# Local attention's probabilities scaled by ScalarE instead of VectorE, with a new table for the order of the work, in a two-layer fp32 trunk

## The chip, the cores and the metric

The kernel runs on one core of a Trainium2 chip. Its engines are TensorE (PE in the profile, with its weight loads as PEld), VectorE (DVE), ScalarE (ACT), GpSimd (POOL) and SyncE (SP), which issues the transfers. The metric is device time in microseconds for one execution, as the median of several runs.

## The reference

Two decoder layers over a sequence of 1024 positions and a width of 1024, all in float32. Each layer normalises, projects once, gives the parts of the projection to four token mixers of 256 channels, normalises their outputs, projects out, adds, and then runs a gated feed-forward part:

```python
h = rmsnorm(x, attn_norm[l])
proj = h @ w_in[l]          # split into the inputs of four mixers
y_a = mla_attention(...)    # causal latent attention, 4 heads, rotary part
y_b = short_gated_conv(...)
y_c = multiscale_pool(...)
y_d = swa_sink_attention(q_sw, k_sw, v_sw, swa_sinks[l], slopes)
...                         # per-group rmsnorm, mixed
x = x + mixed @ w_o[l]
h2 = rmsnorm(x, ffn_norm[l])
gate, up = jnp.split(h2 @ w_gate_up[l], 2, axis=-1)
x = x + (jax.nn.silu(gate) * up) @ w_down[l]
```

The scaling that the change touches is the division in the softmax of `swa_sink_attention`: four heads with two key and value heads, a window of 128 positions in blocks of 128, a bias that falls with distance, and one sink logit per head that takes part in the sum and is then dropped:

```python
p = softmax(concatenate([sc, sink], axis=-1), axis=-1)[..., :-1]
out = einsum('bnkgqs,bnskd->bnqkgd', p, vv)
```

## The kernel before

Everything is kept transposed, channels on partitions, and the 1024 positions are two halves of 512. A float32 product is three products of rounded halves: each operand is split into a high half, a cast by ScalarE (L305, L237 for weights), and a low half, a subtract by VectorE (L306, L238); the helper that issues the three products is at L294, so most matmuls carry that line whatever they belong to. Tiles called `u` live in numbered SBUF buffers (in `u40_2007` the buffer is 40, the tile 2007); `tp`, `tn`, `te`, `sm` are small pools of temporaries; `ps_mm`, `ps_s`, `ps_t`, `ps_pv` are PSUM tiles, where `ps_mm` has two buffers. A matmul that is first to read a buffer's new tile waits for the cast or subtract that wrote it, and that one waits for the last matmul that read the old tile.

The program runs layer by layer: input projection and the mixers (0 to about 430 us in layer 0, 1090 to 1500 in layer 1), the feed-forward's gate and up products (430 to about 815, 1500 to 1805), its down projection (815 to 1090, 1805 to 2022), and a short tail. Gate and up, down and input projections use seven products in place of eight on 2x2 blocks, so their operands are also summed by VectorE and GpSimd, and stored to and loaded from memory by SP.

Places that the prediction speaks of:
- `swa_unit` (L742): one unit is one of two key heads and one block of 128 queries, 32 units in all. TensorE makes the scores of two query heads (L753), VectorE adds the bias and takes the row maxima, ScalarE takes the exponentials and row sums, VectorE adds the sink's share and takes reciprocals, and then the rows `p3` are multiplied by their reciprocals `rs` (L791, two instructions a unit). TensorE transposes the result (L802), it is split by L305 and L306, and multiplied with the values (L814).
- `values()` of the latent attention (L1109 to 1156): four value tiles, each one `ps_mm` tile of 2 x 256 columns, filled by six products and then emptied in two halves by ScalarE (L1155) and VectorE (L1156).
- Key products into `ps_s`, score products (L1223 to 1225), their masking with row maxima on VectorE (L1231), normalisation by sums of squares (L355, L362 to L368, with a load of ScalarE's tables ahead of L362 and L363), accumulation in SBUF (L372), and copies out of PSUM by ScalarE (L458).

What sets the order: the whole program is first recorded, each instruction with its rank. `places` (L2346) groups instructions by engine and written tile, and adds to the rank of a group the number that the table `MOVES` (L2279) holds for it. `arrange` (L2138) then runs through the recorded steps as a list scheduler: an engine takes, of the instructions that it holds to be ready, the one with the lowest place. `order_engines` (L2359) fixes the resulting order on each engine. Each engine works strictly in that order, so an instruction that waits holds up those behind it.

Of the kernel before, what the change touches and what calls it, by code (L numbers as in the profile page):

```python
# [14 lines left out]
AF = mybir.ActivationFunctionType  # L15
ALU = mybir.AluOpType
# [106 lines left out]
def trunk_kernel(ctx: ExitStack, tc: tile.TileContext, ins, out):  # L123
    nc = tc.nc
    act, dve, pe, pool, sp = nc.scalar, nc.vector, nc.tensor, nc.gpsimd, nc.sync
# [450 lines left out]
    for l in range(L):  # L576
# [94 lines left out]
        if l == 0:  # L671
# [15 lines left out]
            if l == 0:  # L687
                enter_norm(1)
                dve.tensor_copy(e_r, cst[:, CC_E : CC_E + P])
                for i in range(L):  # L690
                    for o, c, n in ((nsink, PC_SINK, 4), (nffn, PC_FFN, NK)):
                        dve.tensor_scalar(
                            out=o[:, i * n : i * n + n],
# [48 lines left out]
        def swa_unit(g, i):  # L742
# [47 lines left out]
            for h in range(2):  # L790
                dve.tensor_scalar(  # L791
                    out=p3[:, h, c0:],
                    in0=p3[:, h, c0:],
                    scalar1=rs[:, h : h + 1],
                    scalar2=None,
                    op0=ALU.mult,
                )
# [1340 lines left out]
def arrange(steps, rank=lambda v: v.rank):  # L2138
# [368 lines left out]
```

## Time and profile before

| | |
|---|---|
| median of 3 runs | 2034.13 us (2032.77 to 2035.87) |
| the profiled execution | span 2031.1 us; no other time is given for it |
| mean granted TensorE clock | 0.998 |
| PE busy | 2014.0 us (99%) |
| DVE busy | 1644.2 us (81%) |
| ACT busy | 1030.7 us (51%) |
| POOL busy | 210.7 us (10%) |
| transfers | 320.21 MB |

The span runs from the first to the last instruction of one execution. Busy time is the sum of an engine's instructions; matmul ends are modelled, so that back-to-back matmuls overlap on the page, and a late start shows best as the distance between two starts. In rows of a timeline a bracket such as `[1.79 <-DVE u L1156]` is idle time of the engine ahead of the row and what ended it.

### The profile page before, as it was taken

What the parts mean: (1) busy time and instruction counts of PE and PEld (TensorE: products, weight loads), DVE (VectorE), ACT (ScalarE), POOL (GpSimd) and SP (SyncE); (2) the same over time, 40 slices, a digit from 0 to 9 for tenths busy, and PEclk for the clock granted to TensorE, in tenths of its full rate; (3) what the DMA queues carried; (4) which work ended last, traced back from release to release, by engine and by line L of the source; (5) the groups of instructions that cost most, each with busy time, mean ns of one, the idle gap of its engine ahead of it and who ended that gap; (6) DMA issues with size and microseconds to landing.
All of it is one profiled execution on the core that took longest, in us unless ns stands there. A gap on an engine that the chain in (4) does not pass through costs nothing.

```text
span 2031.1 us, 26457 instructions
## 1 busy us (share of the span) xinstructions
PE 2014.0 (99%) x9378; PEld 1669.4 (82%) x9378; DVE 1644.2 (81%) x2793; ACT 1030.7 (51%) x1803; POOL 210.7 (10%) x212
## 2 busy tenths in 40 slices
PE   9999999999999999999999999999999999999998
PEld 7887888878888888888888878888888888888887
DVE  7889989998888888655778999899977777886555
ACT  7447656763333335443545676667333233355342
POOL 0000000013212213000000000000322222220000
PEclk9999999999999999999999999999999999999999
DMA  5100223346666667875455112231644454497652
GB/s 185 55 27 34 75 87 111 126 141 228 211 217 228 217 232 256 304 241 174 148 176 167 39 41 99 89 127 58 218 161 145 159 182 147 157 325 261 198 175 88
DMA packets 163781, 320.21 MB, mean 158 GB/s; under 512 B 13248, under 2 KB 85056, under 8 KB 163648
## 3 DMA queue, kind: packets, MB, share of 16 engines
q1 hardware_dynamic: 163648, 318.51, 45.6%
q8 instruction: 74, 1.21, 0.2%
q14 instruction: 59, 0.48, 0.1%
HBM read 220.41 MB, written 98.04 MB: 157 GB/s over the span
## 4 chain that ended last, share of the span: by engine, by line
PE 93%; DVE 3%; ACT 2%; DMA 1%; issue 1%; SPq 0%; DVEq 0%; ACTq 0%
PE ps_mm L294 37%; PE ps_s L294 28%; PE ps_t L294 11%; PE ps_pv L294 8%; PE ps_pv L1289 2%; PE ps_t L1277 2%; PE ps_s L1223 1%; PE ps_s L1224 1%; PE ps_s L1225 1%; PE ps_pv L814 1%; PE ps_s L753 1%; PE ps_mm L1109 1%; PE ps_t L802 1%; DVE u L346 1%; DVE u L306 1%
## 5 line engine op out<-in xcount | busy, mean ns | idle before, releaser
L294 PE MATMUL ps_mm<-u,u 128*128 128x512 f32 (+1 forms) x3402 | 856.6, 388 | 2.3 <-ACT u L237 1.3
L294 PEld LDWEIGHTS ps_mm<-u,u 128*128 128x128 f32 x3402 | 621.7, 188 | 126.8 <-issue 3.1
L294 PE MATMUL ps_s<-u,u 128*128 128x512 f32 x2628 | 651.2, 389 | 0.0
L294 PEld LDWEIGHTS ps_s<-u,u 128*128 128x128 f32 x2628 | 492.6, 188 | 104.2 <-DVE te L1796 0.8
L305 ACT CAST u<-u 128x1024 fp32r<-128x1024 f32 (+2 forms) x400 | 344.3, 883 | 412.1 <-PE ps_s L294 82.1
L306 DVE TENSOR_TENSOR u<-u,u 128x1024 fp32r<-128x1024 f32 (+2 forms) x400 | 412.7, 1049 | 165.2 <-ACT u L305 127.3
L172 POOL TENSOR_TENSOR u<-u 128x256 f32<-128x256 f32 x176 | 204.3, 1162 | 743.0 <-DMA u<-in_w_dn 239.2
L294 PE MATMUL ps_t<-u,u 128*128 128x512 f32 (+1 forms) x1142 | 275.1, 378 | 1.2 <-ACT u L305 0.8
L294 PEld LDWEIGHTS ps_t<-u,u 128*128 128x128 f32 x1142 | 205.5, 188 | 42.1 <-DVE u L306 1.3
L294 PE MATMUL ps_pv<-u,u 128*128 128x512 f32 x696 | 172.9, 389 | 0.0
L294 PEld LDWEIGHTS ps_pv<-u,u 128*128 128x128 f32 x696 | 130.5, 188 | 27.5 <-ACT tn L458 0.3
L1604 ACT ACTIVATE tp<-tp 128x512 f32<-128x512 f32 x84 | 53.3, 634 | 117.1 <-DVE tp L372 116.8
L1286 POOL MEMSET u<- 128x128 f32 x32 | 6.2, 220 | 858.8 <-DVE te L372 623.7
L305 ACT CAST u<-ps_t 128x512 fp32r<-128x512 f32 (+4 forms) x136 | 64.9, 507 | 58.7 <-PE ps_t L1277 34.1
L306 DVE TENSOR_TENSOR u<-ps_t,u 128x512 fp32r<-128x512 f32 (+4 forms) x136 | 77.0, 584 | 13.6 <-ACT u L305 12.7
L308 ACT ACTIVATE u<-u,par 128x512 fp32r<-128x512 f32 x100 | 70.0, 719 | 34.0 <-DVE u L372 10.9
L309 DVE SCALAR_TENSOR_TENSOR u<-u,par,u 128x512 fp32r<-128x512 f32 x100 | 73.1, 752 | 4.5 <-ACT u L308 4.4
L1605 DVE TENSOR_TENSOR tp<-tp,u 128x512 f32<-128x512 f32 x84 | 62.6, 745 | 13.2 <-ACT tp L1604 12.7
L340 ACT ACTIVATE tn<-u 128x512 f32<-128x512 f32 (+1 forms) x92 | 53.3, 594 | 39.0 <-DVE u L1882 30.2
L458 ACT COPY tn<-ps_s 128x512 f32<-128x512 f32 x66 | 38.4, 582 | 62.8 <-PE ps_s L294 62.5
L372 DVE TENSOR_TENSOR tp<-tp,u 128x512 f32<-128x512 f32 x80 | 60.9, 761 | 1.1
L1289 PE MATMUL ps_pv<-u,u 128*128 128x512 f32 (+2 forms) x184 | 54.4, 358 | 0.0
(220 smaller groups left out, 2171.9 us busy)
## 6 DMA issues: line engine op xcount, KB each, us to landing
u<-in_w_gu SPq DMA_DIRECT2D x88, 512.0 KB, 3.6
ad<-u SPq DMA_DIRECT2D x154, 256.0 KB, 2.8
u<-ad SPq DMA_DIRECT2D x70, 512.0 KB, 4.9
u<-in_w_dn SPq DMA_DIRECT2D x68, 512.0 KB, 4.9
qd<-u SPq DMA_DIRECT2D x44, 512.0 KB, 3.0
u<-qd SPq DMA_DIRECT2D x32, 512.0 KB, 4.9
u<-in_w_in SPq DMA_DIRECT2D x29, 512.0 KB, 3.5
u<-ws SPq DMA_DIRECT2D x28, 512.0 KB, 3.5
```

Source lines behind the costliest of these rows:

```text
L172: pool.tensor_tensor(out=o, in0=o, in1=u, op=ALU.add)
L294: pe.matmul(o, w, r, start=start and k == 0 and i == 0, stop=stop and k == n - 1 and i == 2, skip_group_check=again,)
L305: act.copy(hi, f)
L306: dve.tensor_tensor(out=lo, in0=f, in1=rd(hi), op=ALU.subtract)
L308: act.activation(hi, f, AF.Copy, scale=gain)
L309: dve.scalar_tensor_tensor(out=lo, in0=f, scalar=gain, in1=rd(hi), op0=ALU.mult, op1=ALU.subtract)
L340: act.activation(q, f, AF.Square)
L372: dve.tensor_tensor(out=o, in0=a, in1=b, op=ALU.mult)
L1277: pe.transpose(p[:, b * P : (b + 1) * P], pr[b][j // 4][:, (j % 4) * P : (j % 4 + 1) * P], ident,)
L1289: pe.matmul(py[:, c0:], v_of(j, h), R.ap(s)[:, c0:], start=j == 0 and n == 0, stop=j == nj - 1 and n == 1,)
L1604: last_silu = act.activation(g, g, AF.Silu)
L1605: dve.tensor_tensor(out=g, in0=g, in1=r, op=ALU.mult)
```

## The change

Two things are changed. In `swa_unit` the rows are multiplied by their reciprocals by a ScalarE activation with the function Copy and a scale per row, in place of VectorE's `tensor_scalar`, 64 instructions in all. And the table `MOVES`, 543 entries before, is replaced by one of 3856 entries that reach over the whole program. The number of matmuls (9352), transfers (830), table loads (11) and all other instructions is unchanged. Lines below the edit are four lower in the changed kernel: L1156 is L1152 there.

```diff
             for h in range(2):
-                dve.tensor_scalar(
-                    out=p3[:, h, c0:],
-                    in0=p3[:, h, c0:],
-                    scalar1=rs[:, h : h + 1],
-                    scalar2=None,
-                    op0=ALU.mult,
+                act.activation(
+                    p3[:, h, c0:], p3[:, h, c0:], AF.Copy, scale=rs[:, h : h + 1]
                 )
...
 MOVES = {
-    3: -1110, 4: -1104, 5: -984, 7: -776, 8: -1105, 14: -914, 15: -964, 16: -307, 18: -279, 20:
...
+    4736: 90, 4737: 227, 4738: -330, 4739: 202, 4740: 163, 4741: 10,
 }
```

What the table does is seen in the engines' orders. First VectorE at the value tiles of layer 0, around 218 to 224 us of the profile before (`ps_mm_2204` and `ps_mm_2216` are the first and second value tile). Before:

```order
L372 TENSOR_TENSOR te_2176<-ps_mm_2148,u30_302 128x512
L342 SCALAR_TENSOR_TENSOR u33_2070<-tn_2252,u33_2070 128x512
L238 TENSOR_TENSOR u21_2120<-u32_2117,u45_2119 128x768
L306 TENSOR_TENSOR u20_2256<-u33_2070,u20_2256 128x512
L372 TENSOR_TENSOR u27_2066<-u27_2066,te_2176 128x512
L1156 TENSOR_TENSOR u32_2203<-ps_mm_2204,u32_2203 128x4x64
L1156 TENSOR_TENSOR u7_2215<-ps_mm_2216,u7_2215 128x4x64
L372 TENSOR_TENSOR te_2192<-ps_s_2185,u39_1403 128x512
L1156 TENSOR_TENSOR u32_2203<-ps_mm_2204,u32_2203 128x4x64
```

Of the change:

```order
L372 TENSOR_TENSOR te_2176<-ps_mm_2148,u30_302 128x512
L342 SCALAR_TENSOR_TENSOR u33_2070<-tn_2252,u33_2070 128x512
L372 TENSOR_TENSOR u27_2066<-u27_2066,te_2176 128x512
L238 TENSOR_TENSOR u21_2120<-u32_2117,u45_2119 128x768
L306 TENSOR_TENSOR u20_2256<-u33_2070,u20_2256 128x512
L1152 TENSOR_TENSOR u7_2215<-ps_mm_2216,u7_2215 128x4x64
L372 TENSOR_TENSOR te_2192<-ps_s_2185,u39_1403 128x512
L1152 TENSOR_TENSOR u7_2215<-ps_mm_2216,u7_2215 128x4x64
L238 TENSOR_TENSOR vlo_2306<-vraw_2303,vhi_2305 128x256
L1152 TENSOR_TENSOR u32_2203<-ps_mm_2204,u32_2203 128x4x64
```

The two tiles were emptied in turn, the first one first; now the second is emptied, both halves, and then the first, whose other half follows three rows further on. In the changed program the third tile has the buffer of the second, and the fourth that of the first.

Second, ScalarE ahead of the feed-forward part of layer 0, around 410 to 418 us. `u24_4292` is the cast of a 128x1024 tile that products of the feed-forward read; the `L362` to `L364` rows normalise. Before:

```order
L362 ACTIVATE tn_4204<-ps_pv_4198 128x512
L305 CAST u22_4281<-tp_4273 128x512
L363 ACT_TABLE_LOAD
L363 ACTIVATE tn_4204<-tn_4204 128x512
L364 ACTIVATE tn_4205<-tn_4204 128x512
L305 CAST u32_2203<-tp_4274 128x512
L305 CAST u28_4285<-tp_4275 128x512
L466 ACTIVATE te_4325<-u29_3436,par_75 128x512
L305 CAST u24_4292<-u42_3928 128x1024
```

Of the change:

```order
L305 CAST u22_4281<-tp_4273 128x512
L362 ACT_TABLE_LOAD
L362 ACTIVATE tn_4204<-ps_pv_4198 128x512
L305 CAST u24_4292<-u42_3928 128x1024
L363 ACT_TABLE_LOAD
L363 ACTIVATE tn_4204<-tn_4204 128x512
L305 CAST u32_2203<-tp_4274 128x512
L364 ACTIVATE tn_4205<-tn_4204 128x512
```

The cast of `u24_4292` moves ahead of the table load of L363; `u32_2203` stands ahead of L364, but behind that cast.

Third, TensorE in the products with the weight halves `u36_2006` (high) and `u40_2007` (low), around 203 to 208 us. `u40_1944`, read by L355, is the tile that buffer 40 held before `u40_2007`. The change has:

```order
L355 MATMUL ps_t_1943<-u40_1944,ones_r_79 128x512
L294 MATMUL ps_mm_2035<-u29_248,u21_1862 128x512 x2
L294 MATMUL ps_mm_2035<-u29_248,u2_1863 128x512
L294 MATMUL ps_mm_2123<-u7_131,u36_2006 128x512 x2
L294 MATMUL ps_mm_2123<-u7_131,u40_2007 128x512
```

and before, the end of that stretch read:

```order
L294 MATMUL ps_mm_2035<-u28_244,u21_1862 128x512
L294 MATMUL ps_mm_2123<-u7_131,u36_2006 128x512 x2
L294 MATMUL ps_mm_2035<-u28_244,u21_1862 128x512
L294 MATMUL ps_mm_2035<-u28_244,u2_1863 128x512
L294 MATMUL ps_mm_2035<-u29_248,u21_1862 128x512 x2
L294 MATMUL ps_mm_2035<-u29_248,u2_1863 128x512
L294 MATMUL ps_mm_2123<-u7_131,u40_2007 128x512
```

The last L355 on `u40_1944` has moved back behind the products that stood after it: it is now six matmuls ahead of the first reader of `u40_2007`, where it had been 22.

507 rows, old and new, of the table MOVES are left out of this document.

## The prediction

> **What bounds the kernel now.** I read the page, then its chain of waits, then the busy times by stage, then the rows around every place where TensorE starts late.
>
> ```profile
> span 2031.1 us, 26457 instructions
> PE 2014.0 (99%) x9378; PEld 1669.4 (82%) x9378; DVE 1644.2 (81%) x2793; ACT 1030.7 (51%) x1803; POOL 210.7 (10%) x212
> ...
> PE 93%; DVE 3%; ACT 2%; DMA 1%; issue 1%; SPq 0%; DVEq 0%; ACTq 0%
> ```
>
> TensorE sets the end: busy for 99% of the span and 93% of the chain. A change that leaves the matmuls as they are, as this one does, can only move the late starts between them. They are counted against the step of an undisturbed run, here from the chain:
>
> ```profile
> 884.36 14.96 PE ps_mm L294 x66
> ```
>
> 14.96 / 66 = 0.2267 us from the start of one 128x512 matmul to the next. The windows by stage (after the length: busy time of PE, PEld, DVE, ACT, POOL; then the granted clock, which is full) show where idle time stands:
>
> ```profile
> 0.00:220.00 220.00, 217.68 (x1043) 180.35 (x1044) 189.27 (x415) 136.03 (x285) 0.55 (x6) 1.00 0.21 74
> 220.00:430.00 210.00, 207.28 (x1027) 171.76 (x1026) 194.48 (x409) 146.38 (x302) 2.69 (x14) 1.00 0.27 97
> 430.00:800.00 370.00, 369.70 (x1628) 304.79 (x1627) 317.54 (x430) 146.26 (x199) 92.49 (x80) 1.00 0.65 223
> 800.00:1100.00 300.00, 300.00 (x1363) 249.06 (x1362) 202.11 (x311) 144.41 (x233) 9.96 (x8) 1.00 0.63 209
> ```
>
> The feed-forward and down-projection of layer 0 (430 to 1100) have 0.30 us of PE idleness: nothing can be won there, only lost. Idle time, 2.3 and 2.7 us, stands in the entry and mixer stages ahead of them.
>
> **The change part by part: the scaling.** It removes 64 VectorE instructions and adds 64 on ScalarE.
>
> ```profile
> L791 DVE TENSOR_SCALAR tp<-tp,sm x64: 273/349/357, 60.8 to 1155.6; 128x256 f32<-128x256 f32 x56, 128x128 f32<-128x128 f32 x8
> ...
> who waited for it (us, times):
> ...
> L410 ACT ACTIVATE u<-u,par x8: 507/513/514, 1937.9 to 2021.3; 128x256 f32<-128x256 f32 x8
> ...
> 50.00:210.00 160.00, 160.00 (x787) 132.19 (x786) 140.06 (x331) 92.72 (x213) 0.00 (x0) 1.00 0.11 37
> 1090.00:1200.00 110.00, 109.97 (x536) 89.44 (x535) 106.94 (x249) 79.46 (x171) 0.00 (x0) 1.00 0.22 71
> ...
> 50.00:210.00 160.00, 9.48 (x32) 1.00 0.11 37
> 1090.00:1200.00 110.00, 6.63 (x22) 1.00 0.22 71
> ```
>
> VectorE sheds 64 x 0.349 = 22 us. The nearest ScalarE row, L410, an activation with a parameter on the same 128x256 shape, takes 0.51 us, so ScalarE takes on at most 64 x 0.51 = 33 us. The last two rows are L791's own share of the two stretches above them. In 1090 to 1200 VectorE falls from 106.94 to 100.3 of 110 us (97% to 91%) and ScalarE rises by 22 x 0.51 to 90.7 (82%); in 50 to 210 they go to 82% and 68%. Neither gets full. PE idles 0.03 us in these 270 us and nobody waited for L791, so alone this is worth little. A modelled matmul end (0.39 us long at a step of 0.2267) hides late starts under about 0.16 us, and those the relief of a 97% engine can shorten: I take 1.0 us won, between 2 us won and the loss of the third rival.
>
> **The order.** The table goes from 543 to 3856 entries; rows move on every engine. These are the late starts that it touches.
>
> ```profile
> 221.15 0.75 PE L355 MATMUL ps_t<-u,ones_r 128*128 128x512 f32 x2
> 223.69 0.36 PE L294 MATMUL ps_mm<-vhi,u 128*128 128x256 f32 x1 [1.79 <-DVE u L1156]
> ...
> 412.76 3.56 PE L294 MATMUL ps_s<-u,u 128*128 128x512 f32 x15
> 417.11 0.73 PE L294 MATMUL ps_t<-u,u 128*128 128x512 f32 x2 [0.79 <-ACT u L305]
> 417.68 0.86 PE L294 MATMUL ps_s<-u,u 128*128 128x512 f32 x3
> 418.68 1.19 PE L294 MATMUL ps_t<-u,u 128*128 128x512 f32 x4
> ...
> 445.12 1.52 PE L294 MATMUL ps_s<-u,u 128*128 128x512 f32 x6
> 446.48 0.61 PE L294 MATMUL ps_t<-u,u 128*128 128x512 f32 x2
> 447.37 0.97 PE L294 MATMUL ps_t<-u,u 128*128 128x512 f32 x3 [0.28 <-DVE u L306]
> ...
> 1416.74 2.20 PE L294 MATMUL ps_s<-u,u 128*128 128x512 f32 x9
> 1419.97 0.73 PE L294 MATMUL ps_mm<-u,u 128*128 128x512 f32 x2 [1.03 <-ACT u L305]
> 1420.54 0.62 PE L294 MATMUL ps_s<-u,u 128*128 128x512 f32 x2
> ```
>
> Start to start, less the steps between: at 221, 2.54 - 2 x 0.2267 = 2.09 us; at 412 to 418, 5.92 - 20 x 0.2267 = 1.39; at 445, 2.25 - 8 x 0.2267 = 0.44; at 1416, 3.23 - 9 x 0.2267 = 1.19. After such a stop the next start is late too (1419.97 to 1420.54 is 0.57 for two steps, 0.11 over); for the two not inside the sums I add 0.2.
>
> *What goes.* At 412 and 1416 the cast of a raw 128x1024 tile stood too far back in ScalarE's queue:
>
> ```profile
> 411.87 1.28 ACT L363 ACT_TABLE_LOAD   x1
> ...
> 414.37 1.13 ACT L305 CAST u<-tp 128x512 fp32r<-128x512 f32 x2
> ...
> 416.03 1.03 ACT L305 CAST u<-u 128x1024 fp32r<-128x1024 f32 x1
> ```
>
> The last row is the cast PE waited for. In the new order it stands ahead of the table load, so it passes 411.87 to 416.03, 4.16 us of work, three times the 1.39 lost: gone. At 1416 the PE rows that read the cast's result stand 60 and more matmuls further behind their neighbours, 13 us: 1.19 gone. At 445 nine ps_mm matmuls, 2.0 us, are put ahead of the one that waited 0.44: gone.
>
> *What stays.* At 221 the two orders look different, but the third value tile is held by the same kind of chain. VectorE began it when the last matmul of the product before had ended, and reached the emptying that PE waited for at the end of the second row:
>
> ```profile
> 218.53 0.69 DVE L372 TENSOR_TENSOR te<-ps_mm,u 128x512 f32<-128x512 f32 x1
> ...
> 223.13 0.42 DVE L1156 TENSOR_TENSOR u<-ps_mm,u 128x256 fp32r<-128x256 f32 x1
> ```
>
> That is 5.02 us. The new order empties the second tile first and gives its buffer to the third: the same queue less one L1156, about 4.7, against the same PE work between (6 key products, two value tiles, two L355). So the third tile gains 0.3, and the fourth now waits for L238, L1156, L306, L1257 and L1156, about 2.1 us, behind 2.0 us of PE work: 0.1 lost. I take 0.2 won of the 2.09.
>
> *What comes new.*
>
> ```profile
> 203.14 0.69 DVE L372 TENSOR_TENSOR u<-u,te 128x512 f32<-128x512 f32 x1
> 203.74 0.30 DVE L1231 CUSTOM_DVE_ANT_0 ps_s<-ps_s,cst 128x128 f32<-128x128 f32 x1
> ...
> 204.84 0.75 DVE L309 SCALAR_TENSOR_TENSOR u<-u,par,u 128x512 fp32r<-128x512 f32 x1
> 205.51 1.22 DVE L238 TENSOR_TENSOR u<-u,u 128x1024 fp32r<-128x1024 f32 x1
> ...
> 1412.63 0.61 ACT L305 CAST u<-tp 128x512 fp32r<-128x512 f32 x1
> ...
> 1089.25 0.59 ACT L458 COPY tn<-ps_mm 128x512 f32<-128x512 f32 x1 [1.29 <-PE ps_mm L294]
> ...
> 1090.36 0.94 PE L294 MATMUL ps_mm<-u,u 128*128 128x512 f32 x3
> ```
>
> - 203: u40_2007, the low half of a weight, is written over u40_1944. From the last reader of the one to the first of the other there were 22 matmuls; there are 6, 1.36 us. In VectorE's queue L372 (0.60 to the next start), the three L1231 (203.74 to 204.84, 1.10) and L238 (1.22) stand between: 2.9 us. Late by up to 1.6, or by 0 if VectorE's first rows run before; I take 1.2.
> - 412 again: the first of the two casts in the 414.37 row, which the product at 417.68 reads, stands behind the moved cast now. It ended at about 415.0; 1.03 more for the moved cast, 0.6 less for L364, which it passes, is 415.4. Its reader comes 6 matmuls (1.36) earlier, and 1.39 of stop ahead of it are gone: 414.9. Late by 0.5, and up to 0.9; I take 0.6.
> - 1090: L458's result was ready at 1089.84 for a product at 1090.36, 0.52 spare. The product comes 4 matmuls earlier (0.5 to 0.9 us) and L458 nine instructions later in its queue. Bounds 0 and 1.0; I take 0.5.
> - 1416 again: the cast at 1412.63, ready at 1413.24, is read by the seventh of the nine ps_s from 1416.74, at 1418.10. The reader moves 26 matmuls (5.9 us) earlier, to 1412.2, the cast two instructions back. Late by 1.0, bounds 0 and 2.2.
> - Tight buffers elsewhere. For each SBUF buffer I counted the matmuls from the last reader of its old tile to the first of its next. Below 12 there were 7 tiles and there are 40; 30 of them lie in the stages without idleness, where there was 1. An old site at distance 8 is inside this row:
>
> ```profile
> 1204.90 6.26 PE L294 MATMUL ps_mm<-u,u 128*128 128x512 f32 x26
> ```
>
> Undisturbed, 26 are 0.39 + 25 x 0.2267 = 6.06: it cost 0.20. The other six old sites show 0.07 together by the same count, so one costs 0.27 / 7 = 0.04, and 33 more 1.3 us; bounds 0 and 33 x 0.44 (the wait at 445) = 14.5.
>
> **Sum.** Gone: 1.39 + 0.44 + 1.19 + 0.2 + 0.2 + 1.0 = 4.4. New: 1.2 + 0.6 + 0.5 + 1.0 + 1.3 = 4.6. The span becomes 2031.1 + 0.2 = 2031.3. The median of the runs shown is 2034.1, 3.0 over the profiled span; with the same 3.0 the forecast is **2034.3 us**, no change.
>
> **Rivals.**
> 1. The new waits hardly come: every release behind them is at its early bound, since VectorE has 22 us less to do and ScalarE half its time free. Then the 4.4 stay won and of the 4.6 no more than 0.4 comes: 2034.1 - 4.0 = 2030.1, and with the 2 us bound of the relief 2029.1. For it: each of the four new waits is a small difference of two sums, while 445 and 1416 have four and ten times the cover they need. Against it: three of the four new places are late by the rows even if nothing else slips.
> 2. Tight buffers decide: slower. Place: 430 to 1100 and 1500 to 1990. At 8 matmuls, 1.81 us, a cast of 1.03 leaves 0.78; one other 128x1024 cast ahead of it in ScalarE's queue uses that up and 0.25 more, and VectorE's subtract, 1.22, waits behind. At 0.25 us for each of 33 sites 8.3 us are lost instead of 1.3: 2034.3 + 7.0 = 2041.3. It passes the margin from about 0.16 us a site. Against it: ScalarE is busy 146.26 of 370 us there.
> 3. ScalarE's longer scaling is late: slower. Each of 32 units takes 2 x (0.51 - 0.35) = 0.32 us more before its transposes; if PE waits in 20 of them, 6.4: 2034.3 + 6.4 = 2040.7. It passes the margin from 12 units. Against it: nobody waited for L791, beside a VectorE that was 97% busy. The Trainium skill (ScalarE: Activation LUTs, Rules for kernel authors) says that a multiply belongs on VectorE rather than ScalarE; the trace agrees on the price of one (0.51 against 0.349 us), and by that rule this rival's time would be the result.
>
> **How the numbers follow.** A difference under 0.2%, 4.07 us, cannot be told from no change: faster is below 2030.06, slower above 2038.2. The forecast has 0.50, its own range 2030.5 to 2038 (new waits at their bounds): 0.02 faster, 0.43 the same, 0.05 slower. Rival 1 has 0.29: 0.24 faster, 0.05 the same. Rival 2 has 0.12: 0.10 slower, 0.02 the same. Rival 3 has 0.05, slower, and 0.04 is left for a late load in the moved DMA queue, slower. Faster 0.26, same 0.50, slower 0.24. The range runs from 2028.5, just past rival 1, to 2039.5, which cuts off the upper half of rivals 2 and 3.
>
> **What the profile after will show.** Right: a wait of about 1.7 us for L1152 (once L1156) near 220 and new PE waits near 203, 412, 1087 and 1412 of 0.5 to 1.5 each, none of the old ones at 416, 446 and 1419; the scaling at about 0.51 us with nobody waiting. Rival 1: PE idleness of 0 to 430 under 3 us, where it was 5.0. Rival 2: over 3 us of PE idleness in 430 to 1100. Rival 3: PE waiting for the scaling or its transposes in 50 to 210. The forecast is wrong if the span leaves 2027 to 2035.

## The result, and the profile after

The changed kernel takes **2066.75 us** (2065.67 to 2070.15, four runs), beside 2033.50 us of the kernel before on the same chip: a ratio of 1.0163, 95% interval 1.0149 to 1.0177. It is slower by 33 us. The forecast was 2034.3 us, no change, in a range that ended at 2039.5: the result lies outside it.

The page of the changed kernel begins:

```profile
span 2068.4 us, 26441 instructions
PE 2029.0 (98%) x9378; PEld 1662.6 (80%) x9378; DVE 1627.1 (79%) x2729; ACT 1051.5 (51%) x1867; POOL 197.2 (10%) x212
```

The shares hardly move, and they are not where to look. VectorE's busy time falls by 17 us and ScalarE's rises by 21, the way that the scaling's move asks; the span grows by 37.3 us (the profiled execution of the change, 2070.15 us, is the longest of its four). TensorE's work is the same, so these are late starts. The busy times of the kernel before from 1500 on, which the prediction did not show (length: busy time of PE, PEld, DVE, ACT, POOL; granted clock; DMA share; GB/s):

```profile
1500.00:1800.00 300.00, 300.00 (x1324) 248.13 (x1323) 231.47 (x304) 107.32 (x148) 70.30 (x61) 1.00 0.48 167
1800.00:2031.00 231.00, 221.53 (x1100) 188.01 (x1098) 137.02 (x184) 95.14 (x135) 9.56 (x8) 0.99 0.59 205
```

and of the changed kernel:

```profile
220.00:430.00 210.00, 206.92 (x1020) 169.30 (x1019) 191.95 (x409) 144.20 (x298) 2.84 (x16) 1.00 0.29 97
430.00:800.00 370.00, 362.58 (x1578) 293.83 (x1577) 305.58 (x414) 139.20 (x191) 89.91 (x80) 1.00 0.63 210
800.00:1100.00 300.00, 295.73 (x1315) 241.93 (x1313) 196.79 (x282) 145.64 (x224) 9.41 (x8) 1.00 0.64 214
1500.00:1800.00 300.00, 299.56 (x1317) 246.36 (x1316) 224.61 (x295) 102.91 (x143) 62.77 (x59) 1.00 0.44 150
1800.00:2068.00 268.00, 252.77 (x1221) 209.73 (x1219) 162.81 (x218) 109.33 (x154) 12.55 (x14) 0.99 0.62 209
```

From 430 to 1100, where TensorE had 0.30 us of idleness, it now has 7.42 + 4.27 = 11.7. The modelled matmul ends hide part of each stop; from start to start, less the undisturbed step, the loss against the kernel before is 3.3 us in 0 to 430, **20.0 in 430 to 1100**, 3.0 in 1100 to 1500 and **11.6 from 1500 on**, 37.9 together. Where a stage is held to end moves the first three by a us or two. About four fifths lie in the feed-forward and down-projection stages.

What ends the idleness there is seen best in one piece of the chain of waits of the changed kernel (start, length, what):

```profile
984.87 2.06 PE ps_s L294 x9
986.93 0.02 issue
986.95 5.44 DMA u<-ad
992.38 0.02 issue
992.41 1.05 ACT u L305
993.46 0.04 issue
993.50 0.50 PE ps_s L294
```

A buffer came free with a product at 986.9; a load into it was issued at once, took 5.44 us, its cast followed within 0.03 us, and the product that reads the cast within 0.04. Nothing in this chain has any cover. In the kernel before the same load (`u24_8596`) landed at 947.72, its cast ended at 948.80 and its first reader started at 964.44, 15.6 us later.

Another piece shows a store in the load's place. Two rows of the changed kernel's timeline:

```profile
451.72 1.04 ACT L305 CAST u<-u 128x1024 fp32r<-128x1024 f32 x1 [6.99 <-DMA ad<-u]
452.81 0.73 PE L294 MATMUL ps_t<-u,u 128*128 128x512 f32 x2 [1.51 <-ACT u L305]
```

and of the kernel before, the same cast:

```profile
444.95 1.05 ACT L305 CAST u<-u 128x1024 fp32r<-128x1024 f32 x1 [2.03 <-DMA ad<-u]
```

The cast writes into a buffer from which a store into `ad` was still reading. In the changed kernel ScalarE is idle for 6.99 us ahead of it: it isn't busy, it waits for a transfer.

For each late start over 0.15 us I followed the waits, and the queue of the waiting engine, back to where the chain began. In the changed kernel 25 begin with a load (18.1 us), 13 with a store (9.5), 14 stand behind a long queue of VectorE or ScalarE work, fourteen steps and more (8.4); before it was 1 load (1.4), 2 stores (0.6), 9 queues (4.3). Where a chain is held to begin is in part a choice; followed in another way, single sums come out up to 4 us different, and the classes keep their order. So of the 38 us lost, 25.6 begin with a transfer and some 4 with a queue. Another 4 are second starts: directly behind a late start of over 0.15 us, 57 starts are themselves 40 to 150 ns late, 5.9 us together, where there were 16 with 1.6. A wider count: of ScalarE's casts that wait on a transfer's semaphore (350 before, 344 after), the median time from the cast's end to its first reader on TensorE was 19.5 us and is 11.8; with less than 1 us there were 13 and there are 54.

### The profile page after: what moved, and what is told of

Same layout as the page of the kernel before. It is cut to its first block, busy times and chain, and to the rows that moved or that the text cites. A ratio compares the mean times of both kernels' runs of the same rounds, so it can differ in the third digit from the quotient of the medians.

```text
span 2068.4 us, 26441 instructions
## 1 busy us (share of the span) xinstructions
PE 2029.0 (98%) x9378; PEld 1662.6 (80%) x9378; DVE 1627.1 (79%) x2729; ACT 1051.5 (51%) x1867; POOL 197.2 (10%) x212
## 4 chain that ended last, share of the span: by engine, by line
PE 42%; DVE 6%; DMA 4%; ACT 1%; issue 1%; SPq 0%; DVEq 0%; ACTq 0%
PE ps_mm L294 15%; PE ps_s L294 13%; PE ps_t L294 5%; PE ps_pv L294 4%; DMA u<-ad 2%; DVE u L306 1%; DMA u<-ws 1%; PE ps_pv L1285 1%; PE ps_t L1273 1%; DVE u L309 1%; ACT u L305 0%; DMA u<-in_w_dn 0%; DMA u<-qd 0%; DMA u<-in_w_o 0%; DMA ad<-u 0%
## 5 line engine op out<-in xcount | busy, mean ns | idle before, releaser
L294 PE MATMUL ps_s<-u,u 128*128 128x512 f32 x2628 | 660.7, 390 | 10.7 <-ACT u L305 7.7
L305 ACT CAST u<-u 128x1024 fp32r<-128x1024 f32 (+2 forms) x400 | 344.3, 880 | 450.1 <-DMA u<-ad 78.5
L306 DVE TENSOR_TENSOR u<-u,u 128x1024 fp32r<-128x1024 f32 (+2 forms) x400 | 408.5, 1039 | 178.3 <-ACT u L305 130.7
L294 PE MATMUL ps_t<-u,u 128*128 128x512 f32 (+1 forms) x1142 | 280.4, 379 | 5.6 <-ACT u L305 3.2
L172 POOL TENSOR_TENSOR u<-u 128x256 f32<-128x256 f32 x176 | 191.1, 1087 | 782.8 <-DMA u<-in_w_dn 417.4
L294 PE MATMUL ps_pv<-u,u 128*128 128x512 f32 x696 | 180.6, 391 | 3.0 <-ACT u L305 2.5
L306 DVE TENSOR_TENSOR u<-ps_t,u 128x512 fp32r<-128x512 f32 (+4 forms) x136 | 76.4, 583 | 15.9 <-ACT u L305 14.9
L305 ACT CAST u<-ps_t 128x512 fp32r<-128x512 f32 (+4 forms) x136 | 64.6, 506 | 32.0 <-PE ps_t L1273 24.8
L1601 DVE TENSOR_TENSOR tp<-tp,u 128x512 f32<-128x512 f32 x84 | 66.4, 796 | 5.4 <-ACT tp L1600 5.1
L372 DVE TENSOR_TENSOR tp<-tp,u 128x512 f32<-128x512 f32 x80 | 63.5, 800 | 0.4
L1475 DVE TENSOR_TENSOR tp<-ps_t,tn 128x512 f32<-128x512 f32 x38 | 26.0, 685 | 36.1 <-PE ps_t L294 34.5
```

The source lines that it names most:

```text
L172: pool.tensor_tensor(out=o, in0=o, in1=u, op=ALU.add)
L294: pe.matmul(o, w, r, start=start and k == 0 and i == 0, stop=stop and k == n - 1 and i == 2, skip_group_check=again,)
L305: act.copy(hi, f)
L306: dve.tensor_tensor(out=lo, in0=f, in1=rd(hi), op=ALU.subtract)
L372: dve.tensor_tensor(out=o, in0=a, in1=b, op=ALU.mult)
L1475: dve.tensor_tensor(out=w.gate, in0=pd, in1=k1, op=ALU.add)
```

## The experiments

Theory A: the new table takes away the cover between transfers and the casts and products behind them. Theory B: the scaling comes late on ScalarE (the prediction's third rival). Theory C, in the first four runs: the new order of the mixers makes the loss. Rival C, from the fifth run on, is another: the casts wait in ScalarE's own queue, however long the transfers are (the prediction's second rival). Each ratio is against the kernel before on the same chip, 2033.07 to 2033.94 us; the chips differ from one group of runs to the next.

### The two parts of the change, apart

`e1_scale_only` has ScalarE's scaling and the old table (its numbers carried to the groups of the same tiles), `e2_table_only` the scaling on VectorE and the new table.

```diff
-                dve.tensor_scalar(
...
+                act.activation(
+                    p3[:, h, c0:], p3[:, h, c0:], AF.Copy, scale=rs[:, h : h + 1]
                 )
```

```diff
 MOVES = {
-    3: -1110, 4: -1104, 5: -984, 7: -776, 8: -1105, 14: -914, 15: -964, 16: -307, 18: -279, 20:
...
+    0: 519, 1: 28, 2: 1105, 3: -1107, 4: -1102, 5: -984, 6: 284, 7: 11, 8: -1104, 9: 1324,
...
 }
```

The first is e1, the second e2, both against the kernel before.

> The scaling moves to ScalarE, the old table stays (its numbers given to the same groups of instructions, since the groups are counted anew). Theory A, the new order lost the cover of its transfers: no change, 2033.5 within 4 us. Theory B, ScalarE's scaling of 0.49 us is late for the transposes: 2045 or more. Theory C, the mixers' order: no change, as A.

> The new table with the scaling still on VectorE. A and C: nearly the whole loss, 2060 to 2068. B: under 2050, since the cause is left out.

Measured: 2043.61 us for the scaling (ratio 1.0049, 1.0032 to 1.0066) and 2111.70 for the table (1.0386, 1.0371 to 1.0402). No theory said either: A and C had 2033.5 within 4 and 2060 to 2068, B 2045 or more and under 2050. Neither part is free, and the parts do not add: 10 + 78 against the change's 33. The reason is that the kernel orders itself at build time by a list scheduler with durations. With other durations on ScalarE and VectorE the same table gives another order: to get from one order of the 9351 matmuls to the other, at least 256 have to move between e1 and the kernel before, and 1020 between e2 and the change (the texts of the last pair have 153 and 668, which is too few). So these two runs are not what they are named after. A clean pair came last, below.

`e3_new_mixers` and `e4_new_ffn` divide the table by place, both with ScalarE's scaling: e3 has the new numbers outside the feed-forward and down-projection and the old ones in them, e4 the other way round. Of the changed kernel's table they replace, in e4 for instance, from its first row on:

```diff
 MOVES = {
-    0: 519, 1: 28, 2: 1105, 3: -1107, 4: -1102, 5: -984, 6: 284, 7: 11, 8: -1104, 9: 1324, 10: -331,
...
+    3: -1110, 4: -1104, 5: -984, 7: -776, 8: -1105, 14: -914, 15: -964, 16: -307, 18: -279,
...
 }
```

> Scaling on ScalarE; the new table for the entry and mixer stages alone, the old one for the feed-forward and down-projection stages. By the late starts of the two profiles (3.4 us more in 0 to 430, 3.0 more in 1100 to 1500) A expects 2040 within 3 us. C expects most of the 33 us, 2055 or more. B expects 2045 or more, as with the scaling alone.

> Scaling on ScalarE; the new table for the feed-forward and down-projection stages alone. By the late starts (20 us more in 430 to 1100, 11.6 more from 1500 on) A expects 2064 within 4 us, with PE waits behind casts that wait for transfers. C expects under 2045. B expects 2045 or more.

Measured: 2055.85 us (1.0107, 1.0092 to 1.0122) and 2080.09 (1.0228, 1.0213 to 1.0243). Against e1 the new mixers cost 12 us, the new feed-forward 36, both together, which is the changed kernel, 23. Theory A missed both, by 16 us each. Theory C had 2055 or more for e3, which came, and under 2045 for e4, which did not; theory B's 2045 or more came in both. So this pair decides nothing by its times alone. The feed-forward's half carries most, as in the trace, but again the parts don't add; that a joint between two orders costs time of its own is likely and not shown. In e4 the late starts behind a load (some 13 us) and behind a store (6 to 9) are most of those of the changed kernel; in e3 they are 3 to 5 and 1.4.

### Longer loads, with the order held

If theory A is right, the new order must be sensitive to how long a transfer takes, and the old one not. `e7` and `e8` make the 70 loads of 512 KB from `ad` out of short pieces; every engine keeps its order to the last instruction.

```diff
-                sp.dma_start(F.ap2(s), ad[c][:, 2 * n * HT : (2 * n + 2) * HT])
+                mid = ad[c][:, (2 * n + 1) * HT - 32 : (2 * n + 1) * HT + 32]
+                sp.dma_start(F.ap2(s).rearrange("p (a c) -> p a c", c=64), mid.unsqueeze(1).to_broadcast([128, 2 * HT // 64, 64]))
```

> The kernel before; each of the 70 loads of 512 KB from ad is made of pieces of 64 columns (256 B) and no longer of whole rows: one slice of 64 columns, from the middle of the two stored tiles, is read 16 times. Bytes landed, waits and the order on every engine are those of before; the values of the other columns are left out. If such a load takes 2 us longer than the 4.9 us of before (how much is read from its trace), theory A expects little here, since 1.4 us of late starts go back to loads and a cast comes well after its load: 0 to 8 us slower, 2034 to 2042 us. Rival C: 0 to 2 us.

> The same loads in pieces in the changed kernel, in its own order. Theory A: 25 places already start late behind a load, and behind 45 loads of ad a cast waits, so each us by which these loads get longer adds 10 us or more, several times what it adds in the kernel before: at 2 us longer 20 to 60 us, 2087 to 2127 us. Rival C: as little as in the kernel before, under 5 us more than 2066.8.

The page's issues of transfers (count, size, median us to landing), of the kernel before and of e7, the same order with pieces:

```profile
u<-ad SPq DMA_DIRECT2D x70, 512.0 KB, 4.9
```

```profile
u<-ad SPq DMA_DIRECT2D x70, 512.0 KB, 6.6
```

and of the changed kernel and of e8:

```profile
u<-ad SPq DMA_DIRECT2D x70, 512.0 KB, 5.2
```

```profile
u<-ad SPq DMA_DIRECT2D x70, 512.0 KB, 6.1
```

Measured: e7 **2033.70 us** (ratio 0.9998, 0.9989 to 1.0008), e8 **2095.88** (1.0302, 1.0287 to 1.0317). In the old order 1.7 us on the median load cost nothing that can be measured; in the new order 0.9 us on the median load cost 29.1 us more than the changed kernel, and its late starts behind loads went from 18.1 to between 34 and 38 us. The loads of `ad`, which alone were changed, stand ahead of 5 late starts with 5.7 us in the changed kernel and of 16 with 23.4 us in e8. The down projection of layer 0 in e7 and then in e8:

```profile
800.00:1100.00 300.00, 300.00 (x1361) 249.10 (x1360) 201.46 (x310) 143.62 (x232) 8.66 (x8) 1.00 0.78 211
```

```profile
800.00:1100.00 300.00, 284.12 (x1221) 229.90 (x1220) 187.13 (x245) 134.51 (x187) 9.01 (x8) 0.98 0.77 204
```

The same load on the DMA engines (0.78 and 0.77, where the same windows had 0.63 and 0.64), the same work, and TensorE idle for 0 and for 15.9 us. Theory A had 0 to 8 us and 20 to 60. Rival C expected under 5 us in either order, so it falls as the main cause.

### Shorter stores, with the order held

The other direction. A first pair halved the stores into `ad` by writing 64 of 128 rows:

```diff
-                sp.dma_start(ad_of(c, g), v)
+                sp.dma_start(ad_of(c, g)[:64], v[:64])
...
-                sp.dma_start(F.ap2(s), ad[c][:, 2 * n * HT : (2 * n + 2) * HT])
+                sp.dma_start(F.ap2(s), twice(ad[c][:64, 2 * n * HT : (2 * n + 2) * HT]))
```

> The changed kernel; every store into ad, the DRAM copy of the activations that the down-projection reads, writes 64 of its 128 rows, and the loads of ad read these 64 rows twice. The order on every engine is the changed kernel's; what the reference wants of the other rows is left out. Theory A (in the new order casts stand close behind transfers, whose cover it took away): at 13 places of the changed kernel's trace, 9.5 us of late starts, a cast waits for a store that still reads the buffer. A store of half the size lands 1 to 2 us sooner, so most of these go, and some of the late starts behind loads too, since less is moved: 5 to 10 us faster than the changed kernel, 2057 to 2062 us. Rival C (the casts wait in their own engine's queue, however long the transfers are): within 2 us of 2066.8.

> The same halved stores in the kernel before, in its own order. Theory A: there only 0.6 us of late starts go back to a store, so 0 to 2 us faster than before: 2032 to 2034 us. If the stores' traffic itself slowed TensorE, it would gain as much as the changed kernel does from the same edit. Rival C: the same, 2032 to 2034.

Measured: 2681.80 us (1.3186, 1.3166 to 1.3205) and 2638.07 (1.2971, 1.2951 to 1.2990). Both missed by 600 us, and for a reason that has nothing to do with stores: the loads written this way crawl (last section). ScalarE's waits in e5, where the casts of L305 have line 308 (us in total, times, longest):

```profile
ACT u L308 <- DMA u<-ad: 716.1, 72, 23.8
```

The pair says nothing of the stores. It does show where cover ends for both orders: with loads as slow as that, old and new lose alike, 604 and 615 us.

A second pair halves the stores by columns (`kept` takes 256 of the 512 columns), and the loads keep 128 rows:

```diff
-                sp.dma_start(ad_of(c, g), v)
+                sp.dma_start(kept(ad_of(c, g), g), kept(v, g))
...
-                sp.dma_start(F.ap2(s), ad[c][:, 2 * n * HT : (2 * n + 2) * HT])
+                mid = ad[c][:, 2 * n * HT + HT // 2 : 2 * n * HT + HT // 2 + HT]
+                sp.dma_start(F.ap2(s).rearrange("p (a c) -> p a c", a=2), twice(mid))
```

> The stores of ad halved once more, this time without touching the number of rows, so that a load keeps its 512 KB in rows of 2 KB pieces. The changed kernel, its order on every engine; each store into ad writes 256 of its 512 columns in all 128 rows, the loads of ad read the written 512 columns of a pair of tiles twice; the values of the other columns are left out. Theory A (casts stand close behind transfers in the new order): the 9.5 us of late starts behind stores go in part, a store of 128 KB landing 0.5 to 2 us sooner: 3 to 9 us faster than the changed kernel, 2058 to 2064 us. Rival C (ScalarE's own queue of casts): within 2 us of 2066.8. If a load in pieces of 2 KB is slower than in rows of 4 KB, the run says nothing of stores.

> The same edit in the kernel before, in its own order. Theory A: 0.6 us of late starts behind stores, so 0 to 1.5 us faster: 2032.5 to 2034.5. Rival C: the same.

Measured: e9 2062.35 us (1.0146, 1.0129 to 1.0163), 4.4 us less than the changed kernel, with runs from 2060.91 to 2064.81 where those of the change start at 2065.67 (the interval of the ratio overlaps the change's, so the gain is likely and not certain); e10 2032.18 (0.9997, 0.9988 to 1.0007), no change. The stores of e9 land in 2.3 us (median), where those of the change took 3.2; the median load of `ad` takes 5.1 us there, as in the change. Late starts behind a store fell from 13 places and 9.5 us to 8 and 4.6. Theory A had 3 to 9 us, so the run fits it, in the lower half of its range. Not all of the 9.5 could go: some 5.5 of them stand behind stores into `ad`, now down to 2.5, and most of the rest behind stores into `ws`, which the edit leaves as they are.

### The scaling and the order, cleanly apart

The last pair fixes the orders by force: the scheduler plans with the scalings where that order had them, and afterwards the 64 instructions are moved to the other engine's list, at the time at which the plan had them. All other instructions keep their places on every engine. The edit of e11; e12 moves them from ACT to DVE in the same way:

```diff
+    queues = arrange(places(steps_of(tc)), lambda v: v.place)
+    moved = [v for v in queues["DVE"] if scales_row(v.ins[0])]
+    queues["DVE"] = [v for v in queues["DVE"] if v not in moved]
+    queues["ACT"] = sorted(queues["ACT"] + moved, key=lambda v: v.start)
```

> The scaling alone, cleaner than in e1_scale_only, where the planner, given other durations, also moved 153 matmuls: here every engine keeps the old order to the last instruction; the 64 scalings leave VectorE's list and stand in ScalarE's at the time at which the plan had them. Theory A: the scaling costs nothing, 2032 to 2036 us, and the 10 us of e1_scale_only came from the moved instructions. Theory B (the scaling comes late on ScalarE): 2038 to 2046 us, with new waits of TensorE between 60 and 210 and between 1090 and 1160 whose chain runs through the scalings.

> The other corner: every engine keeps the changed kernel's order to the last instruction; the 64 scalings leave ScalarE's list and stand in VectorE's at the time at which the plan had them. Theory A: the order alone makes the loss: 2062 to 2072 us (in e2_table_only, 2112 us, the planner had moved 668 matmuls besides). Theory B: some 5 to 10 us of the loss belong to the scaling on ScalarE and go: 2055 to 2062 us.

| median, us | scaling on VectorE | scaling on ScalarE |
|---|---|---|
| old order | 2033.07 | 2040.79 (e11; 1.0039, 1.0024 to 1.0054) |
| new order | 2072.55 (e12; 1.0195, 1.0173 to 1.0217) | 2066.75 (the change) |

The order alone costs 39 us with the scaling on VectorE and 26 with it on ScalarE. The scaling alone costs **7.7 us in the old order** (5 to 11 by the interval). In the new order, which was made with it, no cost shows: e12 is 5.8 us slower than the change, but its four runs spread from 2067.8 to 2077.4, and the intervals of the two ratios overlap, so a saving is not shown either. So theory B is true in the old order and fails in the new one, where it had 2055 to 2062. The rows of ScalarE and TensorE in e11 at one unit:

```profile
1157.56 0.51 ACT L791 ACTIVATE tp<-tp,sm 128x256 f32<-128x256 f32 x1
1158.10 0.58 ACT L305 CAST u<-ps_t 128x512 fp32r<-128x512 f32 x1
1158.58 0.48 ACT L776 ACTIVATE tp<-ps_s,sm 128x256 f32<-128x256 f32 x1
1159.04 0.51 ACT L791 ACTIVATE tp<-tp,sm 128x256 f32<-128x256 f32 x1
```

```profile
1158.30 0.27 PE L798 MATMUL ps_t<-cst,tp 128*128 128x128 f32 x1
1159.60 0.55 PE L798 MATMUL ps_t<-cst,tp 128*128 128x128 f32 x3 [1.03 <-ACT tp L791]
```

The second scaling of the unit starts 1.48 us after the first, behind a cast and an exponential, and TensorE, after one transpose of four, waits for it. What ended the idle time before all L798, in e11 (us, times; matmuls and weight loads together):

```profile
  ACT tp L791: 8.6, 20
```

Of the 20, 16 are weight loads and four are matmuls. By start to start the transposes are 5.7 us late in all, in about a dozen of the 32 units. In the changed kernel no row waits for L791.

## Why the prediction was wrong, point by point

**The place of the bound** was right: TensorE sets the end, nothing could be won in 430 to 1100, only lost.

**The scaling, "1.0 us won".** Duration right (0.499 us median in e11 and in the change, forecast 0.51), effect wrong in the old order: 7.7 us lost. The prediction read "nobody waited for L791" as slack. That row says only that the slack was not negative: how much there was, it does not say, and the cast and the exponential between the two scalings above, a microsecond, used it up. The third rival had the mechanism, with 20 late units and 2040.7 us, and was given 0.05. That e11 has 20 waits and 2040.8 is luck in both numbers: its waits are those of about a dozen units, up to 1.2 us a unit and not 0.32. The rule that stood beside that rival, of the Trainium skill (ScalarE: Activation LUTs, Rules for kernel authors), has a multiply belong on VectorE; in the old order the runs agree, by 7.7 us; in the new order they don't decide.

**What goes.** The late starts at 412 and 1416 went, 2.6 us, as worked out. The one at 445 did not: the prediction put nine matmuls ahead of the reader and took the 0.44 us as gone. The row that it quoted there, `[0.28 <-DVE u L306]`, was the end of a chain whose beginning, two steps back, is the store in the row at 444.95 above. A store doesn't move with the matmuls: it is issued when its data are ready. In the new order it landed at 451.65, and the place costs 1.67 + 0.52 us.

**What stays.** At 221 the forecast was 2.09 less 0.2. The changed kernel loses 0.61, 1.12 and 0.54 from 223.6 to 229.6, 2.27: the 0.2 did not come. The rest came in size, but as three waits and not as the one of about 1.7 us that was to be seen.

**What comes new,** in the mixers. The rows of TensorE in the changed kernel:

```profile
207.21 0.84 PE L294 MATMUL ps_mm<-u,u 128*128 128x512 f32 x3
208.26 0.73 PE L294 MATMUL ps_mm<-u,u 128*128 128x512 f32 x2 [0.20 <-ACT u L237]
209.51 1.19 PE L294 MATMUL ps_mm<-u,u 128*128 128x512 f32 x4 [0.53 <-DVE u L238]
...
417.80 1.75 PE L294 MATMUL ps_s<-u,u 128*128 128x512 f32 x7
420.74 0.50 PE L294 MATMUL ps_s<-u,u 128*128 128x512 f32 x1 [1.19 <-ACT u L305]
...
1113.08 0.63 PE L753 MATMUL ps_s<-u,u 128*128 128x256 f32 x4
1114.14 0.73 PE L294 MATMUL ps_mm<-u,u 128*128 128x512 f32 x2 [0.43 <-ACT tn L458]
...
1435.70 2.43 PE L294 MATMUL ps_s<-u,u 128*128 128x512 f32 x10
1438.87 1.42 PE L294 MATMUL ps_s<-u,u 128*128 128x512 f32 x5 [0.74 <-ACT u L305]
```

By start to start: 1.17 at 207 (forecast 1.2), 0.91 at 1436 (1.0), 0.58 at 1113 (0.5; four 256-column products take 0.48), and 1.35 at 420 (0.6, bound 0.9). Four of four places came, three at their price, though at 207 a part of it, 0.37, is a wait for a cast (L237) that the forecast did not have. At 420 the queue ahead of the cast came out as worked out. Its rows in the changed kernel:

```profile
417.19 1.04 ACT L305 CAST u<-u 128x1024 fp32r<-128x1024 f32 x1
418.25 1.28 ACT L363 ACT_TABLE_LOAD   x1
419.55 0.63 ACT L363 ACTIVATE tn<-tn 128x512 f32<-128x512 f32 x1
420.08 0.60 ACT L305 CAST u<-tp 128x512 fp32r<-128x512 f32 x1
```

The table load stands ahead of that cast in the old order too (411.87 in the prediction's rows), so it is not what was missed. What differs is when ScalarE came there:

```profile
410.49 0.62 ACT L305 CAST u<-tp 128x512 fp32r<-128x512 f32 x1 [0.64 <-DVE tp L475]
```

From this row to the end of the cast waited for it takes 10.2 us; from the same row of the kernel before, at 404.99, it took 10.0. ScalarE came to it 5.5 us later, behind VectorE. The cast ended at 420.68, 5.3 us behind the 415.4 worked out, while its reader, had it not waited, would have started at 419.39, 4.5 behind the 414.9: the difference, 0.8, is what the term lacks.

Where the prediction followed single rows it was good to a few tenths. That it called the mixers a small gain, and they lost some 6 us, comes from places that it did not look at, loads of `ws` among them: 0.80, 0.92 and 0.69 us at 1100.6, 1117.9 and 1127.5.

**"Tight buffers elsewhere", 1.3 us: this is the step that failed.** It was the only loss that the sum had for the stages without idleness, and those stages lost some 30 us. It saw the right sign, 40 tight buffers in place of 7, and 30 of the 40 in those stages where there was 1. What it took for cover was wrong. It counted the matmuls between the last reader of a buffer and the first reader of its next content, and asked whether a cast of 1.03 us fits between. But what has to fit is the transfer too: the load that fills the raw tile after its buffer came free, or the store that must have read a buffer before the cast may write it. These take 3 to 9 us, not 1, and they stand elsewhere. By the same count the changed kernel has 43 tight sites, and four of them start late, 3.7 us together, three of these in the stages without idleness (3 us): there the price was low, but not by much. Of the 25.4 us of late starts over 0.15 us in those stages, 19.6 stand at 26 places where 13 matmuls or more lie between the two readers (75 at 452.81, 43 at 484.65, 89 at 665.51), places that the prediction priced at nothing. The upper bound, 0.44 us a site from the wait at 445, was a transfer's wait, taken for a cast's. The second rival had the right stages (its sign, over 3 us of idleness in 430 to 1100, came: 11.7) with the wrong mechanism, and so the wrong size, 0.25 us a site. Nearest to what happened was the case with the least text, "a late load in the moved DMA queue", 0.04.

Where that cover went can be read in part from the kernel's own plan: `arrange` lets a transfer land at `max(t + 1400, wire) + size / 330 + 600` ns, 3.6 us for 512 KB on a free wire. The traces have medians of 4.9 and 5.2 us for the loads of `ad`, and the chain of the changed kernel holds a weight load of this size that took 9.24 us. An order that looks free of waits under such a plan would have waits in the trace wherever it leaves less than the difference. That the new table was chosen this way is an argument, not shown by a run.

**What stays open.** About 12 of the 38 us are not traced to a transfer: some 4 us of queues on VectorE and ScalarE, some 4 us of second starts, which follow the same stops, and the rest in small pieces. No run took the waits behind loads away, only made them longer; that loads alone cost 18 us in the change rests on the trace and on the response to longer ones.

## What to carry to other kernels

An order is only as good as the cover of its slowest links: for each wait ahead of the bounding engine follow the chain back until it reaches something that didn't wait, and if that is a transfer, take the time from its landing to the reader, not the matmuls between two readers of a buffer. "Nobody waited for it" is a sign and no size: before an instruction is made longer or moved to a busier engine, measure from its end to its reader's start. And parts of a change that both feed a scheduler cannot be tested one by one through it: fix the order of all engines, then move one thing.

## What the runs showed of the hardware

A load's speed hung on how its access pattern was written. In e5 and e6 a load reads 64 rows twice, as a pattern of 2 x 64 rows. The transfers of e5 between 900 and 960 us, in slices of 1.5 us (busy share of the 16 DMA engines in tenths, then GB/s):

```profile
DMA  1145148786311572111111111112882111149921
GB/s 55 49 188 221 53 85 254 199 196 176 123 48 50 98 289 82 52 52 52 52 49 55 49 52 52 52 52 71 264 273 98 49 49 49 53 141 277 246 60 49
```

For stretches of 16 us one tenth of the engines is busy and 49 to 55 GB/s move, where other slices reach 289; at 50 GB/s, 512 KB take 10.5 us. The Trainium skill (DMA: Bandwidth & Descriptors, Why a DMA increments its semaphore by 16 and not by 1) says that a copy is spread over the largest number of engines, up to 16, that divides the slowest dimension of both sides; by that rule these loads have 2 of 16 engines, and the trace agrees with its tenth. The loads of e9 read the same bytes twice too, but with 128 rows outermost, and land in 5.1 us: reading twice is not what costs.

Pieces of 256 B in place of 4 KB rows raised the share of the DMA engines from 0.63 to 0.78 at the same 209 and 211 GB/s.

TensorE's granted clock fell where it starved. In e5:

```profile
800.00:1100.00 300.00, 137.94 (x484) 106.58 (x482) 70.35 (x81) 50.85 (x63) 9.29 (x8) 0.70 0.30 98
```

The clock is 0.70 at 138 us of work in 300, and 0.98 in e8's 284 of 300; in the changed kernel, whose late starts are at most 1.9 us, the windows above have 1.00, the last one 0.99. Its 37 us are waits alone; e5 lost some of its 615 to slower matmuls: 311 of its 128x512 matmuls have 0.42 us to the next start, where the undisturbed step is 0.2267 and the changed kernel has 8 such.
